# A decoder block on one core: a fourth step of eight by seven products in 15 wide blocks, one of the weight sums by an adding transfer, PSUM banks in pairs

## The chip, the core and the metric

The kernel runs on one core of a Trainium2 chip. The metric is the device time of one execution in microseconds, the median of several runs. All inputs and weights lie in HBM when it starts and the output is in HBM when it ends.

## The reference

One layer of a decoder on 256 positions with 2048 features, all in float32. `w_in` has 17408 columns, and the feed-forward part has 5632 hidden features.

```python
a = rmsnorm(h, norm_mix_pre)
q_a, k_a, v_a, q_r, f_r, i_r, g_r, gate_a, gate_r = split_columns(a @ w_in)
attn  = ...   # dilated window attention, three groups, mixed by their softmax denominators
r_out = ...   # gated linear recurrence, normed per head, times silu(g_r)
y = sigmoid(gate_a) * (attn @ w_attn_branch) + sigmoid(gate_r) * (r_out @ w_hgrn_branch)
h = h + rmsnorm(y @ w_mix_out, norm_mix_post)
a = rmsnorm(h, norm_ffn_pre)
gt, up = split(a @ w_ffn_gate_up)
h = h + rmsnorm((silu(gt) * up) @ w_ffn_down, norm_ffn_post)
```

## The kernel before

All products are made in float32r. To keep float32 accuracy each operand is split into a high part (ACT copies it to float32r) and a low part (VectorE subtracts the high part from the original), and a product is three matmuls: high by high, high by low, low by high. Every weight is used for one pass over the 256 positions, so it has to be loaded (SP), split (ACT and VectorE) and multiplied (PE) once, and the program is one long list of such steps, `seq`. Three raw buffers (`N_RAW`) and three buffers of high parts (`N_SPLIT`) turn round; while PE works on step n, `ahead(n)` emits the split of step n + 2 (`AHEAD`) and then the load that reuses the raw buffer of step n + 2, which is that of step n + 5.

The columns that need no rotation are handled in wide blocks (`Wide`, made by `add_seven`): eight of `w_in` (two column groups of 512 each: the gates, the values, the recurrence's input), two of `w_mix_out`, ten of `w_ffn_gate_up` (512 gate columns with their 512 up columns) and two of `w_ffn_down`. A wide block has two sides of 128 positions and two groups of 512 columns, so four outputs, called (0,0), (0,1), (1,0) and (1,1) by side and group. One step of a block takes 256 rows of the weights, loaded by two transfers of 512 KB, one for each group. It is a product of two matrices of two by two parts. A step by eight makes the eight products of parts, 24 matmuls of 512 columns. A step by seven makes it in the way of Strassen and Winograd with seven products, 21 matmuls: three go straight into an output, four go into shared sums called p1, p5, p6 and p7, which have banks of their own. It needs four sums of the activations (`pair_sums`, made once for each pair of rows, `x7` and `h7`) and four of the weights (made at every such step on VectorE, `sum`), and both the sums and three of the weights' parts have to be split. When the last step by seven of a block is done, `gather` combines the four shared sums into four tiles `e`; when the block is done, the evacuation adds the outputs to them (lines 674, 1106, 1327 and 1374), applies the activation, and stores the result to HBM (`kept`, from the queue of POOL) or turns it (`turn_act`, eight transposes on PE).

The list `EIGHT` gives the order of a block's eight steps as pairs of row index and kind (1 is by seven): three are by seven in each of the 18 blocks of `w_in` and gate_up, and the last step is by eight. Outputs and shared sums take four banks each; the next block swaps the two groups of banks (`flip`). PE, ACT, VectorE and POOL run their instructions in the order in which the program emits them.

Of the kernel before, what the change touches and what calls it, by code (L numbers as in the profile page):

```python
# [19 lines left out]
P = 128  # L20
# [19 lines left out]
DOWN = [[(m, m in by7) for m in range(KF // 2)] for by7 in (range(4, 20, 3), range(3, 19, 3))]  # L40

N_RAW, N_SPLIT, AHEAD, WARM, BRIDGE, LATER = 3, 3, 2, 8, 6, 16
# [21 lines left out]
class Wide:  # L64
# [7 lines left out]
    def __init__(self, w, cols, order, xs, seven, evac, prep=None, pre=None, post=None, turn=None):  # L72
        self.w, self.cols, self.order, self.xs, self.seven = w, cols, order, xs, seven
        self.evac, self.prep, self.pre, self.post, self.turn = evac, prep, pre, post, turn
        self.last7 = max((i for i, (m, s) in enumerate(order) if s), default=None)
        self.steps = len(order)
        self.bank, self.open, self.rest, self.flip, self.at = {}, set(), None, False, {}


class Step:  # L80
# [5 lines left out]
    def __init__(self, block, i, unit, half):  # L86
        self.block, self.i, self.unit, self.half = block, i, unit, half
        self.raw = self.parts = None
        self.home = None
# [4 lines left out]
def tile_hybrid_block(ctx: ExitStack, tc: tile.TileContext, t, out):  # L94
# [7 lines left out]
    accp = ctx.enter_context(tc.tile_pool(name="accp", bufs=4, space=PSUM))  # L102
    auxp = ctx.enter_context(tc.tile_pool(name="auxp", bufs=4, space=PSUM))
# [14 lines left out]

    def aux():
        return auxp.tile([P, 512], F32, tag="aux", name=nm("aux"))  # L120

    def acc_bank():
        return accp.tile([P, 512], F32, tag="acc", name=nm("acc"))
# [4 lines left out]
    def eslot(s="e"):  # L128
        return p3(s, F32, 512, 6, "e")
# [91 lines left out]
    def add_seven(*args, flip, **kw):  # L221
        b = Wide(*args, **kw)
        b.flip = flip
# [23 lines left out]
    def load(u, half):  # L247
# [9 lines left out]
        if type(b) is Wide:  # L257
            m = b.order[i][0]
            for g, col in enumerate(b.cols):
# [4 lines left out]
                )  # L264
            return
# [18 lines left out]
    def sumslot(dtype=F32R):  # L284
        return p3("sum", dtype, 2048, 1)
# [4 lines left out]
    def split(st, only=None):  # L290
        if type(st.block) is Wide:
            split_wide(st)
# [35 lines left out]
    def split_wide(st):  # L328
# [6 lines left out]
        if not by7:  # L335
            nc.scalar.activation(hi, raw, AF.Copy)  # L336
            next(prep, None)
            nc.vector.tensor_sub(lo, raw, hi.bitcast(F32))  # L338
            st.parts = hi, lo
            return  # L340
        s, d = sumslot(F32), raw[:, 512:]
        nc.vector.tensor_sub(  # L342
            s[:, :1024].rearrange("p (a c) -> p a c", a=2),
            raw[:, 512:1536].rearrange("p (a c) -> p a c", a=2),
            raw[:, None, :512].to_broadcast([P, 2, 512]),
        )
        nc.scalar.activation(hi[:, :1024], s[:, :1024], AF.Copy)  # L347
        nc.vector.tensor_add(s[:, 1024:1536], raw[:, 512:1024], s[:, 512:1024])
        nc.vector.tensor_sub(s[:, 1536:], raw[:, 1536:], s[:, 1024:1536])  # L349
        nc.scalar.activation(hi[:, 1024:], s[:, 1024:], AF.Copy)  # L350
        next(prep, None)
        dhi, dlo = (p3(x, F32R, 1536, 1) for x in ("dh", "dl"))
        nc.scalar.activation(dhi, d, AF.Copy)  # L353
        for x in (slice(0, 2048),) if b.prep else (slice(0, 1024), slice(1024, 2048)):
            nc.vector.tensor_sub(lo[:, x], s[:, x], hi[:, x].bitcast(F32))  # L355
        next(prep, None)
        nc.vector.tensor_sub(dlo, d, dhi.bitcast(F32))  # L357
        st.parts = hi, lo, dhi, dlo

    def multiply_wide(st, sides=(0, 1), groups=(0, 1)):  # L360
# [3 lines left out]
        def bank(key):  # L364

            if key not in b.bank:
                b.bank[key] = aux() if b.flip == (type(key) is not tuple) else acc_bank()
            return b.bank[key]

        def prod(key, x, w, j, last=False):  # L370
            ps = bank(key)
# [16 lines left out]
        t, d, sums = w[:2], w[2:], b.seven(m)  # L388
        last = i == b.last7
        prod((0, 1), act_of(0, 1), d, 2)  # L390
        prod((0, 0), sums(3), d, 0)
        prod("p1", act_of(0, 0), d, 1, last)
        prod("p6", sums(1), t, 2, last)
        prod("p5", sums(0), t, 1, last)
        prod("p7", sums(2), t, 0, last)
        prod((1, 1), act_of(1, 1), t, 3)

    def gather(b):

        e = {k: p3("e", F32, 512, 6) for k in ((0, 1), (1, 1), (0, 0), (1, 0))}  # L400
        x = b.bank
        nc.scalar.activation(e[0, 1], x["p1"], AF.Copy)
        nc.vector.tensor_add(e[1, 1], x["p6"], e[0, 1])
        nc.vector.tensor_add(e[0, 0], x["p5"], e[1, 1])
        nc.vector.tensor_add(e[1, 0], x["p7"], e[0, 0])
        nc.vector.tensor_add(e[1, 1], x["p7"], e[1, 1])
        b.rest = e

    def seven_sums(f, dst):

        s = ptile("s").rearrange("p (n t) -> p n t", n=4)
        a11, a12, a21, a22 = f[:, 0, :P], f[:, 1, :P], f[:, 0, P:], f[:, 1, P:]
        for o, x, c, y in ((0, a21, -1.0, a22), (1, s[:, 0, :], -1.0, a11)):
            nc.vector.scalar_tensor_tensor(
                out=s[:, o, :], in0=x, scalar=c, in1=y, op0=OP.mult, op1=OP.subtract
            )
        nc.vector.tensor_sub(s[:, 2, :], a11, a21)
        nc.vector.tensor_sub(s[:, 3, :], a12, s[:, 1, :])
# [142 lines left out]
    def flush(q):  # L561
        while q:
# [107 lines left out]
    def evac_kept(key, fn):  # L670
        def go(b):
            dst, at = keep(key, 1024), [(0, 0), (0, 1), (1, 0), (1, 1)]
            for k in at:
                nc.vector.tensor_add(b.rest[k], b.bank[k], b.rest[k])
            for s, g in at:
                e = b.rest[s, g]
# [940 lines left out]
```

## Time and profile before

| what | value |
|---|---|
| median of 3 runs | 1701.86 us (1701.73 to 1702.48) |
| span of the profiled execution, first to last instruction | 1699.6 us |
| PE busy | 1689.1 us (99%) |
| DVE busy | 1423.5 us (84%) |
| ACT busy | 908.5 us (53%) |
| POOL busy | 40.5 us (2%) |
| mean granted clock of TensorE | 0.998 |
| DMA | 344.77 MB, 203 GB/s on average |

The time of a run holds a little more than the span of a profile, which counts from the first to the last instruction; the profiled execution has no time of its own beside its span. The profile names engines PE (matmuls), PEld (weight loads of PE), DVE (VectorE), ACT (ScalarE), POOL (GpSimd) and SP (whose queue issues the loads). A group is a line of the program with the tile written and the tiles read. All matmuls have one line, that of the helper `mm`.

### The profile page before, as it was taken

The numbers are of one execution on the slowest core, as the hardware profiler recorded it, in microseconds if no ns is written. First come the engines' busy times: TensorE is split into PE (matmuls) and PEld (weight loads), VectorE is DVE, ScalarE is ACT, GpSimd is POOL, SyncE is SP. The second block draws the span as 40 slices with busy tenths as digits, with TensorE's granted clock in tenths as the row PEclk, the third lists the DMA queues.
The fourth block names the chain that finished last, engine by engine and source line by source line (L and its number), as shares of the span: only waits on it lengthen the run. The fifth ranks groups of instructions, "written<-read, shape, count | busy, mean of one in ns | idle before, by whom it ended". The sixth has DMA issues, their size and how long they took to land.

```text
span 1699.6 us, 21507 instructions
## 1 busy us (share of the span) xinstructions
PE 1689.1 (99%) x8265; PEld 1420.0 (84%) x8265; DVE 1423.5 (84%) x1604; ACT 908.5 (53%) x1023; POOL 40.5 (2%) x72
## 2 busy tenths in 40 slices
PE   9999999999999999999999999999999999999997
PEld 7888888888888888888888888888888888888886
DVE  6998888886887987776668889888888888898988
ACT  6655555554535434544445575555555555565663
POOL 0000000001000000000000000000000000000000
PEclk9999999999999999999999999999999999999999
DMA  8666666667546555565457646555555555656653
GB/s 288 220 231 232 232 232 233 228 229 258 180 149 196 188 174 175 173 216 168 154 179 249 237 147 223 198 198 198 198 198 198 198 198 198 221 195 212 200 198 114
DMA packets 206614, 344.77 MB, mean 203 GB/s; under 512 B 10960, under 2 KB 77568, under 8 KB 206512
## 3 DMA queue, kind: packets, MB, share of 16 engines
q1 hardware_dynamic: 198208, 317.89, 55.7%
q0 software_dynamic: 5680, 19.60, 3.3%
q10 hardware_dynamic: 2624, 5.92, 1.0%
q8 instruction: 64, 1.05, 0.2%
q14 instruction: 38, 0.31, 0.1%
HBM read 331.83 MB, written 11.53 MB: 202 GB/s over the span
## 4 chain that ended last, share of the span: by engine, by line
PE 98%; DVE 1%; ACT 0%; issue 0%; DVEq 0%; ACTq 0%
PE acc L135 61%; PE aux L135 35%; PE aux L833 0%; PE aux L501 0%; PE acc L1295 0%; DVE fz L1422 0%; PE aux L1295 0%; PE aux L489 0%; ACT junk L1378 0%; DVE e L1374 0%; DVE w L302 0%; DVE wl L338 0%; PE aux L1033 0%; PE acc L1158 0%; DVE g L758 0%
## 5 line engine op out<-in xcount | busy, mean ns | idle before, releaser
L338 DVE TENSOR_TENSOR wl<-raw,w 128x2048 fp32r<-128x2048 f32 x134 | 306.8, 2289 | 92.3 <-ACT w L336 90.9
L135 PE MATMUL acc<-xT,w 128*128 128x256 f32 (+1 forms) x2048 | 369.8, 339 | 0.0
L135 PEld LDWEIGHTS acc<-xT,w 128*128 128x128 f32 x2048 | 312.0, 188 | 43.8
L302 DVE TENSOR_TENSOR w<-raw,w 128x1024 fp32r<-128x1024 f32 (+1 forms) x191 | 232.5, 1218 | 136.0 <-ACT w L301 135.1
L336 ACT ACTIVATE w<-raw 128x2048 fp32r<-128x2048 f32 x134 | 256.1, 1911 | 149.3 <-PE aux L135 62.6
L301 ACT ACTIVATE w<-raw 128x1024 fp32r<-128x1024 f32 (+1 forms) x191 | 200.9, 1053 | 230.2 <-PE acc L135 187.8
L135 PE MATMUL acc<-w,hT 128*128 128x512 f32 x598 | 175.5, 390 | 0.0
L347 ACT ACTIVATE w<-sum 128x1024 fp32r<-128x1024 f32 x70 | 74.4, 1063 | 186.5 <-DVE sum L342 186.5
L355 DVE TENSOR_TENSOR wl<-sum,w 128x1024 fp32r<-128x1024 f32 (+1 forms) x128 | 168.8, 1321 | 0.0
L135 PE MATMUL acc<-w,xT 128*128 128x512 f32 x536 | 155.1, 392 | 0.0
L135 PE MATMUL aux<-w,hT 128*128 128x512 f32 x430 | 135.7, 389 | 0.0
L135 PEld LDWEIGHTS acc<-w,hT 128*128 128x128 f32 x598 | 111.7, 188 | 23.2 <-DVE w L302 0.2
L357 DVE TENSOR_TENSOR dl<-raw,dh 128x1536 fp32r<-128x1536 f32 x70 | 123.0, 1758 | 8.8 <-ACT dh L353 7.2
L135 PEld LDWEIGHTS acc<-w,xT 128*128 128x128 f32 x536 | 99.9, 188 | 20.9 <-DVE w L302 0.3
L135 PE MATMUL aux<-w,xT 128*128 128x512 f32 x344 | 108.5, 389 | 0.0
L353 ACT ACTIVATE dh<-raw 128x1536 fp32r<-128x1536 f32 x70 | 103.1, 1473 | 0.0
L135 PEld LDWEIGHTS aux<-w,hT 128*128 128x128 f32 x430 | 80.7, 188 | 16.8
L135 PE MATMUL acc<-wl,hT 128*128 128x512 f32 x227 | 86.9, 390 | 0.0
L350 ACT ACTIVATE w<-sum 128x1024 fp32r<-128x1024 f32 x70 | 74.4, 1062 | 21.8 <-DVE sum L349 21.8
L342 DVE TENSOR_TENSOR sum<-raw 128x1024 f32<-128x1024 f32 x70 | 85.2, 1217 | 0.0
L135 PE MATMUL aux<-wl,hT 128*128 128x512 f32 x215 | 83.6, 389 | 0.0
L135 PE MATMUL aux<-w,a 128*128 128x512 f32 x268 | 83.6, 389 | 0.0
(293 smaller groups left out, 2776.8 us busy)
## 6 DMA issues: line engine op xcount, KB each, us to landing
raw<-in_w_in SPq DMA_DIRECT2D x271, 512.0 KB, 4.6
raw<-in_w_ffn_gate_up SPq DMA_DIRECT2D x176, 512.0 KB, 4.4
raw<-in_w_ffn_down SPq DMA_DIRECT2D x88, 512.0 KB, 4.8
raw<-in_w_mix_out SPq DMA_DIRECT2D x32, 512.0 KB, 5.3
kept<-e POOLq DMA_DIRECT2D x32, 256.0 KB, 4.2
raw<-in_w_hgrn_branch SPq DMA_DIRECT2D x16, 512.0 KB, 4.9
raw<-in_w_attn_branch SPq DMA_DIRECT2D x16, 512.0 KB, 4.5
v<-kept POOLq DMA_DIRECT2D x8, 512.0 KB, 5.7
```

The source lines that it names most:

```text
L135: nc.tensor.matmul(ps, lhsT, rhs, start=start, stop=stop, skip_group_check=True)
L301: nc.scalar.activation(wh[:, k], raw[:, k], AF.Copy)
L302: nc.vector.tensor_sub(wl[:, k], raw[:, k], wh[:, k].bitcast(F32))
L336: nc.scalar.activation(hi, raw, AF.Copy)
L338: nc.vector.tensor_sub(lo, raw, hi.bitcast(F32))
L342: nc.vector.tensor_sub(s[:, :1024].rearrange("p (a c) -> p a c", a=2), raw[:, 512:1536].rearrange("p (a c) -> p a c", a=2), raw[:, None, : ...
L347: nc.scalar.activation(hi[:, :1024], s[:, :1024], AF.Copy)
L350: nc.scalar.activation(hi[:, 1024:], s[:, 1024:], AF.Copy)
L353: nc.scalar.activation(dhi, d, AF.Copy)
L355: nc.vector.tensor_sub(lo[:, x], s[:, x], hi[:, x].bitcast(F32))
L357: nc.vector.tensor_sub(dlo, d, dhi.bitcast(F32))
```

## The change

Fifteen of the 18 blocks of `w_in` and gate_up get four steps by seven and four by eight in turn, and so end with a step by seven. The first and last of `w_in` and the first of gate_up keep three. Such a last step makes its shared products first and its outputs last; what is emitted at its end (gather, the end sums) stands ahead of the low part of the step after next.

The step by seven is written anew. Of the four sums of weights one is formed while loading: POOL issues a transfer that adds 256 KB of the first group's rows onto the first 512 columns of the raw buffer, after SP's load of that group has landed. VectorE forms the other three (512 columns and twice 512). The raw buffer is then split like that of a step by eight, and the three sums are split in the step after, out of single buffers `sum`, `dh` and `dl`. The transposes of a finished block stand between two products of a step by seven. Shared sums and outputs are allocated as pairs of banks, and gather, end sums, activations and copies take two banks in one instruction where they can. The steps by seven of the `w_mix_out` and `w_ffn_down` blocks take the new form too, with as many of them as before.

```diff
-X7 = H7 = (0, 1, 2)
+X7, H7 = tuple(range(4)), tuple(range(4))
-EIGHT = [(3, 0), (4, 0), (0, 1), (5, 0), (1, 1), (6, 0), (2, 1), (7, 0)]
+EARLY = [order(x) for x in ["88787878"] + ["87878787"] * 6 + ["88787878"]]
+FFN = [order(x) for x in ["88787878"] + ["87878787"] * 8 + ["87878787"]]
+PAIRS = ((0, 0), (0, 1)), ((1, 0), (1, 1)), ("p1", "p6"), ("p5", "p7")
...
+    def pair_of(n):
+        return banks(n, 2).tile([P, 2, 512], F32, tag=n, name=nm(n))
...
+    def four_e():
+        return p3("e", F32, 2048, 1).rearrange("p (n c) -> p n c", n=4)
...
     def load(u, half):
...
             for g, col in enumerate(b.cols):
...
+                if g == 0 and by7:
+                    rows = b.w[(2 * m + 1) * P : (2 * m + 2) * P, col : col + 512]
+                    nc.gpsimd.dma_start(raw[:, :512], rows, accum_op=OP.add)
...
     def split_wide(st):
...
+        nc.scalar.activation(hi, raw, AF.Copy)
+        yield
         next(prep, None)
-        dhi, dlo = (p3(x, F32R, 1536, 1) for x in ("dh", "dl"))
-        nc.scalar.activation(dhi, d, AF.Copy)
-        for x in (slice(0, 2048),) if b.prep else (slice(0, 1024), slice(1024, 2048)):
-            nc.vector.tensor_sub(lo[:, x], s[:, x], hi[:, x].bitcast(F32))
+        if by7:
+            w = raw.rearrange("p (n c) -> p n c", n=4)
+            flat = p3("sum", F32, 1536, 1)
+            d = flat.rearrange("p (n c) -> p n c", n=3)
+            nc.vector.tensor_sub(d[:, 0], w[:, 0], w[:, 2])
+            nc.vector.tensor_sub(
+                d[:, 1:], w[:, 1:4:2], d[:, 0:1].to_broadcast([P, 2, 512])
+            )
+            st.rest = split_sums(st, flat, prep)
+        yield
+        nc.vector.tensor_sub(lo, raw, hi.bitcast(F32))
+
+    def split_sums(st, flat, prep):
+        hi, lo = (p3(x, F32R, 1536, 1) for x in ("dh", "dl"))
+        nc.scalar.activation(hi, flat, AF.Copy)
+        yield
         next(prep, None)
-        nc.vector.tensor_sub(dlo, d, dhi.bitcast(F32))
-        st.parts = hi, lo, dhi, dlo
+        nc.vector.tensor_sub(lo, flat, hi.bitcast(F32))
+        st.parts += hi, lo
...
     def multiply_wide(st, sides=(0, 1), groups=(0, 1)):
...
-        prod((0, 1), act_of(0, 1), d, 2)
-        prod((0, 0), sums(3), d, 0)
-        prod("p1", act_of(0, 0), d, 1, last)
-        prod("p6", sums(1), t, 2, last)
-        prod("p5", sums(0), t, 1, last)
-        prod("p7", sums(2), t, 0, last)
-        prod((1, 1), act_of(1, 1), t, 3)
+        outs = (
+            lambda: prod((0, 1), act_of(0, 1), w, 3, st.last),
+            lambda: prod((0, 0), sums(3), w, 1, st.last),
+            lambda: prod((1, 1), act_of(1, 1), d, 2, st.last),
+        )
+        turn, at = None, (0, 0, 4)
+        if st.last:
+            at = 4, 4, 4
+        elif st.between:
+            turn, at = st.between(), (0, 0, 2)
+        shared = (
+            ("p1", act_of(0, 0), w, 2), ("p6", sums(2), d, 0),
+            ("p5", sums(1), d, 1), ("p7", sums(0), w, 0),
+        )
...
     def gather(b):
+        e, x = four_e(), b.bank
+        nc.scalar.activation(e[:, 1], x["p1"], AF.Copy)
+        nc.vector.tensor_add(e[:, 3], x["p6"], e[:, 1])
+        nc.vector.tensor_add(e[:, 0], x["p5"], e[:, 3])
+        nc.vector.tensor_sub(
+            e[:, 2:], e[:, 0:4:3], x["p7"][:, None, :].to_broadcast([P, 2, 512])
+        )
...
     def evac_ffn(b):
...
+        nc.vector.tensor_mul(e[:, 1:4:2], e[:, 1:4:2], e[:, 0:4:2])
...
         if n >= 2:
...
+            late = type(b) is Wide and i == b.last7 == b.steps - 1
+            if not late:
+                rest()
...
         if st.last:
             evacs.append(b.evac(b))
             advance(evacs)
+            if late:
+                rest()
```

In `ahead` the emission for step n is now: the high part of the sums of step n + 1, the high part of step n + 2, at a block's first step two parts of the evacuation before, the low part of the sums of n + 1, the weight sums of n + 2, its low part and the load (`rest`).

The first place is VectorE's queue where one gate_up block before follows another. In the names `raw` holds loaded weights, `w` their high and `wl` their low part, `e` the tiles of the block that ends, `aux` and `acc` the banks:

```order
L403 TENSOR_TENSOR e_8811<-acc_8667,e_8810 128x512
L404 TENSOR_TENSOR e_8812<-acc_8671,e_8811 128x512
L405 TENSOR_TENSOR e_8813<-acc_8675,e_8812 128x512
L406 TENSOR_TENSOR e_8811<-acc_8675,e_8811 128x512
L338 TENSOR_TENSOR wl_8820<-raw_8727,w_8819 128x2048
L1327 TENSOR_TENSOR e_8812<-aux_8568,e_8812 128x512
L1327 TENSOR_TENSOR e_8810<-aux_8575,e_8810 128x512
L1327 TENSOR_TENSOR e_8813<-aux_8582,e_8813 128x512
L1327 TENSOR_TENSOR e_8811<-aux_8589,e_8811 128x512
L342 TENSOR_TENSOR sum_8858<-raw_8755 128x1024
```

There a low part stands between gather and end sums, and the block's last step and the next one's first are by eight. The same place of the changed kernel, where `dl` is the low part of the three sums:

```order
L375 TENSOR_TENSOR sum_9283<-raw_9185 128x512
L376 TENSOR_TENSOR sum_9283<-raw_9185,sum_9283 128x1024
L452 TENSOR_TENSOR e_9307<-acc_9084,e_9307 128x512
L453 TENSOR_TENSOR e_9307<-acc_9103,e_9307 128x512
L454 TENSOR_TENSOR e_9307<-e_9307,acc_9103 128x1024
L463 TENSOR_TENSOR e_9307<-aux_9040,e_9307 128x1024
L463 TENSOR_TENSOR e_9307<-aux_9053,e_9307 128x1024
L381 TENSOR_TENSOR wl_9281<-raw_9185,w_9280 128x2048
L1391 TENSOR_TENSOR e_9307<-e_9307 128x2x512
L389 TENSOR_TENSOR dl_9319<-sum_9283,dh_9318 128x1536
L381 TENSOR_TENSOR wl_9322<-raw_9220,w_9321 128x2048
```

The low part of the step after next (`wl_9281`, from `raw_9185`, the next block's second step) has moved behind gather and both end sums, and the weight sums of the same step stand ahead of them.

The second place is PE at the end of such a block, from its last shared product (p7, bank `aux_8810`) to the first product of the next block:

```order
L164 MATMUL aux_8810<-w_8920,so_8427 128x512
L164 MATMUL aux_8810<-wl_8921,so_8427 128x512
L164 MATMUL aux_8810<-w_8920,so_8427 128x512
L164 MATMUL acc_8747<-w_8920,hT_7888 128x512
L164 MATMUL acc_8747<-wl_8921,hT_7888 128x512
L164 MATMUL acc_8747<-w_8920,hT_7888 128x512
L164 MATMUL acc_8747<-w_8920,so_8427 128x512
L164 MATMUL acc_8747<-wl_8921,so_8427 128x512
L164 MATMUL acc_8747<-w_8920,so_8427 128x512
L164 MATMUL acc_8760<-dh_8951,hT_7888 128x512
L164 MATMUL acc_8760<-dl_8952,hT_7888 128x512
L164 MATMUL acc_8760<-dh_8951,hT_7888 128x512
```

Three outputs of three matmuls each now stand between the last shared product and the next block, which writes its outputs to the banks of the shared sums.

More of the change, by code (lines that the diff above doesn't have):

```diff
@@ L362, in multiply_wide, with prod @@
         m, by7 = b.order[i]
-        def bank(key):
+        def prod(key, x, w, j, last=False):
             if key not in b.bank:
[L367 to L371, printed above, removed]
+                side = "aux" if b.flip == (type(key) is not tuple) else "acc"
+                if b.whole:
+                    keys = next(k for k in PAIRS if key in k)
+                    pair = b.bank[keys] = pair_of(side)
+                    b.bank.update((k, pair[:, n, :]) for n, k in enumerate(keys))
+                else:
+                    b.bank[key] = bank_of(side)
+            ps = b.bank[key]
             wh, wl = (v[:, j * 512 : (j + 1) * 512] for v in w)
@@ new lines, in multiply_wide @@
+        turn, at = None, (0, 0, 4)
[7 more added lines that the diff above has]
+        )
+        for n in range(5):
+            for out, k in zip(outs, at):
+                if k == n:
+                    out()
+            if n < 4:
+                prod(*shared[n], last)
+            if n == 0 and turn:
+                turn()
@@ L561, in flush @@
     def flush(q):
+        q = deque(q) if type(q) is list else q
         while q:
@@ L1289, in turn_act, with turn_into @@
         act_t.append(dst)
+        side = "aux" if b.flip else "acc"
+        pair = pair_of(side) if b.whole else [bank_of(side) for _ in range(2)]
+        return lambda: turn_into(dst, pair, u, b.whole)
+    def turn_into(dst, pair, u, whole):
         for i in range(2):
-            ps = aux() if b.flip else acc_bank()
+            ps = pair[:, i, :] if whole else pair[i]
             for kk in range(2):
@@ L1390, in evac_down @@
         parts = [(j, i) for i in range(2) for j in range(2)]
-        for j, i in parts:
-            down_sum(j, i, b)
+        add_up(b)
         yield
@@ L1529, in tile_hybrid_block @@
         if type(b) is Wide:
+            if i == b.turn and b.order[i][1]:
+                st.between = lambda: turn_act(turns.popleft(), b) if turns else None
             multiply_wide(st)
@@ L1537, in tile_hybrid_block @@
         if n < 2:
-            ahead(n)
+            ahead(n)()
         advance(evacs)
```

204 lines of the change are left out of this document (107 added, 97 removed).

## The prediction

> **What bounds the kernel now.** I read the page first, then the list of waits, the chain in order of time, and the stages of the wide blocks.
>
> ```profile
> span 1699.6 us, 21507 instructions
> PE 1689.1 (99%) x8265; PEld 1420.0 (84%) x8265; DVE 1423.5 (84%) x1604; ACT 908.5 (53%) x1023; POOL 40.5 (2%) x72
> PE 98%; DVE 1%; ACT 0%; issue 0%; DVEq 0%; ACTq 0%
> ```
>
> TensorE is busy 99% of the span and is 98% of the chain that ended last. The timed runs have a median of 1701.86, so 2.3 us lie around this span; I work on the span and add them back. The waits of PE alone are two:
>
> ```profile
> PE aux L135 <- DVE warm L159: 1.2, 1, 1.2
> PE aux L135 <- DVE wl L338: 0.6, 1, 0.6
> ```
>
> So nothing else holds it, and what a stage costs is its count of matmuls times their pace. The chain gives the pace (start, length, engine, count), first for a w_in block, then for a gate_up block:
>
> ```profile
> 97.94 12.24 PE acc L135 x54
> 139.42 12.24 PE aux L135 x54
> ...
> 1416.41 10.88 PE acc L135 x48
> 1427.29 0.87 PE aux L1295 x8
> 1458.78 21.76 PE aux L135 x96
> ```
>
> 12.24 / 54 is 0.2267 us for a matmul of 512 columns. A block before has 5 steps of 24 and 3 of 21, 183 in all: 41.48 us, exactly the distance from 97.94 to 139.42. A gate_up block adds the 8 transposes (0.87): 42.36, against 42.37 from 1416.41 to 1458.78. The blocks run without a gap. VectorE is next:
>
> ```profile
> 181.00:222.00 41.00, 41.00 (x183) 33.94 (x182) 35.77 (x32) 22.55 (x19) 2.17 (x4) 1.00 0.67 231
> 1160.00:1201.00 41.00, 41.00 (x187) 34.03 (x186) 36.10 (x33) 22.96 (x19) 0.00 (x0) 1.00 0.56 191
> ```
>
> The columns are span, PE, PEld, DVE, ACT and POOL busy, clock, DMA share, GB/s. VectorE works 36 of 41 us there, which leaves some 5 us a block; ACT is half idle and the clock is full.
>
> **What the change takes from PE.** In 15 of the 18 wide blocks a fourth step goes by seven products. That is 15 x 3 = 45 matmuls fewer; the instruction order has 45 fewer of 512 columns and all else on PE in the same number. 45 x 0.2267 = **10.2 us off**. A w_in block becomes 40.81 us and a gate_up block 41.68.
>
> **What it does to VectorE.** The rows:
>
> ```profile
> L338 DVE TENSOR_TENSOR wl<-raw,w 128x2048 fp32r<-128x2048 f32 x134 | 306.8, 2289 | 92.3 <-ACT w L336 90.9
> L357 DVE TENSOR_TENSOR dl<-raw,dh 128x1536 fp32r<-128x1536 f32 x70 | 123.0, 1758 | 8.8 <-ACT dh L353 7.2
> 1208.55 2.43 DVE L355 TENSOR_TENSOR wl<-sum,w 128x1024 fp32r<-128x1024 f32 x2
> L342 DVE TENSOR_TENSOR sum<-raw 128x1024 f32<-128x1024 f32 x70 | 85.2, 1217 | 0.0
> L348 DVE TENSOR_TENSOR sum<-raw,sum 128x512 f32<-128x512 f32 x70 | 48.4, 692 | 2.4
> L1327 DVE TENSOR_TENSOR e<-aux,e 128x512 f32<-128x512 f32 x20 | 12.4, 682 | 0.0
> L1333 DVE SCALAR_TENSOR_TENSOR e<-e,r2c,e 128x512 f32<-128x512 f32 x20 | 14.1, 746 | 0.0
> ```
>
> A seven step had sums of 1217 + 692 + 692 ns, a low part of 2 x 1.22 and one of 1.76, 6.8 us; one addition now goes to the DMA and it has 692 + 1217 + 2289 + 1758 ns = 5.96. A block before costs 5 x 2.29 + 3 x 6.8 = 31.9, after 4 x 2.29 + 4 x 5.96 = 33.0; gather and end sums shrink from eight 512-wide operations (5.5) to two of 512 and three of 1024 (5.0). So VectorE gets about 0.6 us more in a block that is 0.7 shorter, some 4 us remain free, and on average it does not become the bound. What decides is the order at the seam between two blocks.
>
> **The seam.** Thirteen blocks that end with a seven step are followed by a block whose second step is one too. Put t = 0 where PE starts the last step (L) of a gate_up block; PE's next steps S0 to S6 then start at 4.76, 10.20, 15.83, 21.27, 26.03, 31.47 and 36.23, the next L at 41.67. More rows, of ACT and of VectorE in order of time:
>
> ```profile
> L336 ACT ACTIVATE w<-raw 128x2048 fp32r<-128x2048 f32 x134 | 256.1, 1911 | 149.3 <-PE aux L135 62.6 <-PE acc L135 61.3 <-issue 25.3
> L353 ACT ACTIVATE dh<-raw 128x1536 fp32r<-128x1536 f32 x70 | 103.1, 1473 | 0.0
> L402 ACT ACTIVATE e<-aux 128x512 f32<-128x512 f32 x11 | 6.6, 599 | 1.7 <-PE aux L135 0.9
> 1199.37 0.69 DVE L404 TENSOR_TENSOR e<-aux,e 128x512 f32<-128x512 f32 x1
> 1200.17 0.69 DVE L405 TENSOR_TENSOR e<-aux,e 128x512 f32<-128x512 f32 x1
> 1211.14 1.76 DVE L357 TENSOR_TENSOR dl<-raw,dh 128x1536 fp32r<-128x1536 f32 x1 [0.15 <-ACT dh L353]
> ```
>
> ACT splits S1's weights when S6 has left their slot, 0.1 to 2.0, and copies p1 until 2.6. On VectorE the two weight sums of S1 hide under that. Its gather starts at 2.65; dependent operations start 0.8 apart, so 3.45, 4.25, and the 1024-wide one ends at 5.5. Two end sums of 1.22: 7.95. S1's low part, now queued behind all of these: 10.25. PE wants it for its second matmul of S1, at 10.43. Then the product of gate and up (bounded by twice 0.746; I take 1.22): 11.5, and the low part of the sums: 13.25, wanted after nine matmuls, the transposes and one more, at 13.34. Nothing has more than 0.2 us to spare and a hand-over costs up to 0.15 (the last row). I take a stall of 0.15 at each seam: 13 x 0.15 = **2.0 us on**; in the 5 of w_in, with neither product nor transposes, it is the first of these two limits alone.
>
> What is hidden has this cover: PE's S0 needs the first pair of banks at 4.76 (its gather step is over at 3.45) and the second at 7.5 (free at 5.5). Where a block with pairs is followed by one with single banks, all four must be free at S0: 5.5 against 4.76, **0.7 us on**, once; the other changes of pool stand behind steps that are long over (bounds 0 and 0.7 each). SP's load of S4 waits behind the delayed low part, until 10.25, and the load of S5 stands behind it; both land before their use. On POOL the stores of kept, which wait for ACT's end activations, stand ahead of the adding transfer of S5, whose load is not out yet. The other edits (scale of the up half dropped, table load moved, fewer and wider evictions) touch engines with slack: 0.
>
> **The adding transfer** is not in the trace. The nearest rows: a load pair of SP, then 256 KB stores and 512 KB loads from POOL's queue, each with its landing time:
>
> ```profile
> L261 SPq DMA_DIRECT2D raw<-in_w_ffn_gate_up x2: 367/419/471, 1170.6 to 1171.0; - x2
> DMA to landing us min/median/max: 3.6/4.0/4.5
> ...
> L678 POOL DMA_DIRECT2D kept<-e x32: 540/540/552, 98.7 to 390.2; - x32
> DMA to landing us min/median/max: 2.8/4.2/5.9
> ...
> L668 POOL DMA_DIRECT2D v<-kept x8: 704/716/731, 393.5 to 659.4; - x8
> DMA to landing us min/median/max: 4.1/6.0/9.2
> ```
>
> It is 256 KB on POOL's queue, so its bounds are 2.8 and 9.2 us and I take 4.2, the median of its own size and queue. Call it a. It starts when the first load of the pair has landed (3.6). The Trainium skill, "DMA: Bandwidth & Descriptors", Anatomy of one DMA, puts such a transfer at 2.0 us plus bytes over 436 GB/s, which makes an estimate of 2.6 us for this one; the row of stores does not agree, and by either the sum is the same.
>
> When must it be there? S5's slot is freed by S2's low part (after 13.25, so 15.55). Load and a: 19.2 + a. Then S5's high part 1.91, low part 2.29, the low part of its sums 1.76, S6's low part 2.29: 27.45 + a, or 31.6 where that is later: PE releases the one buffer of sums at 26.03, and 1.47 + 1.76 + 2.29 stand behind it. That frees the slot of the next S1, whose load and a end at 31.15 + 2a. ACT wants it at 41.8. So a costs nothing up to 5.3, and 2 us at each seam for every us beyond. In w_in, without product and transposes, the limit comes out at 5.5. At 4.2 there is 1.1 us of room, so **0**.
>
> Sum: 1699.6 - 10.2 + 2.0 + 0.7 = 1692.1, and with the 2.3 us around it **1694.4 us**.
>
> **Rivals.** A measurement of this kernel can tell 0.2%, 3.4 us, from no change.
>
> Slower: *the adding transfer lands late*. It reads 256 KB from memory and another 256 KB from its destination, so it may behave like the 512 KB loads of the third row, a = 6.0, their median. Then the 8 seams of gate_up stall 2 x 0.7 = 1.4 us each and the 5 of w_in 2 x 0.5 = 1.0: 16.2 us, which swallow the small stalls: 1699.6 - 10.2 + 0.7 + 16.2 + 2.3 = 1708.6. It loses from a = 5.75 on, where 13 seams give back the 9.5 us that are left. For it: half of those loads took over 6.0, and S5's transfer runs beside the load of S6. Against it: half of the stores of its size landed within 4.2 and the worst in 5.9, and only 256 KB come from HBM. The Trainium skill, "Collectives: The Full Stack", The bandwidth ceiling, says of the adding step of a collective that it runs at half the rate of a copy, because it reads two sources; that is this rival, and no run here shows it yet. Chance 0.18.
>
> No change: *VectorE's operations over two banks are slow*. No row has one. If a 1024-wide one costs two of 512 (1.38 for 1.22), the four of the seam add 0.64 us, and the stall is 0.15 + 0.64 less 0.15 of room, 0.64 each: 8.3 us instead of 2.0, 1700.7. Against it: 512 from a bank takes 682, from SBUF 692. Chance 0.10.
>
> Full gain: no seam stalls, 1699.6 - 10.2 + 2.3 = 1691.7 or slightly less. Chance 0.08. The forecast, 1692 to 1698, has 0.64.
>
> **Numbers.** Faster is the forecast and the full gain, 0.72; the same 0.10; slower 0.18. The range goes from 1690, a little below the full gain, to 1706, a = 5.9 by the slope above; outside lies the late transfer with little else.
>
> **What would show it.** PE with 45 matmuls fewer; blocks 40.8 and 41.7 us apart in the chain, plus 0 to 0.3; in PE's waits the low parts of S1 (L381, L389) a few times, tenths of a us each; adding transfers landing in 3 to 5 us; VectorE at about 37 us of 41. I am wrong if PE waits over 0.7 us at a seam, and by the late transfer if those waits lead through ACT or VectorE to the queue of POOL with landings near 6 us.

## The result, and the profile after

The changed kernel takes **1746.23 us** (1741.95 to 1749.39, 4 runs) against 1702.17 (1701.73 to 1702.74): a ratio of 1.0258, 95% interval [1.0246, 1.0271]. It is slower by 44 us where 1694.4 was forecast, and far outside the range. The profiled execution took 1745.72 us, its span is 1743.9.

The page of the changed kernel: the span, the engines, then the chain that ended last by engine and by line.

```profile
span 1743.9 us, 21581 instructions
PE 1695.9 (97%) x8220; PEld 1414.6 (81%) x8220; DVE 1416.8 (81%) x1443; ACT 914.8 (52%) x943; POOL 105.3 (6%) x141
PE 54%; DMA 16%; DVE 10%; issue 3%; ACT 2%; POOLq 0%; DVEq 0%; SPq 0%; ACTq 0%
```

PE has the 45 matmuls fewer (8220 for 8265), and VectorE's share fell from 84% to 81%, so it is not full. But the chain that ended last, PE for 98% of the span before, is now PE for 54% and DMA for 16%. PE's waits (total, times, longest) say where it stood still:

```profile
PE aux L164 <- DVE e L452: 15.3, 7, 3.4
PE acc L164 <- DVE e L452: 11.9, 6, 5.2
PE acc L164 <- DVE wl L381: 5.9, 7, 1.5
PE aux L164 <- DVE wl L381: 3.1, 5, 0.8
```

7 + 6 is 13, the number of seams. At each, S0's matmuls wait for the banks that the gather (L452) empties, and then some for S1's low part (L381). VectorE's and ACT's operations only pass on a delay. The chain in order of time (start, length) through one seam of gate_up shows whose it is:

```profile
1143.76 0.70 DVE e L452
...
1156.17 0.61 DVE sum L375
...
1160.84 3.27 DMA raw<-in_w_ffn_gate_up
...
1166.78 0.70 DVE sum L375
...
1173.42 1.56 DVE wl L381
1174.99 4.95 DMA raw<-in_w_ffn_gate_up
...
1180.15 0.59 issue
1180.75 5.51 DMA raw<-in_w_ffn_gate_up
...
1186.41 1.92 ACT w L368
1188.34 0.49 ACT e L451
...
1188.85 0.70 DVE e L452
```

S6's low part ends at 1174.98 and frees the raw buffer of the next block's S1. Its load takes 4.95, POOL starts the adding transfer 0.8 later, that takes 5.51, and only then can ACT make S1's high part. The copy of p1 (L451) stands behind that on ACT, and the gather behind the copy: this is why a late S1 is seen as S0 waiting for a bank. The chain cuts S5's transfer (1160.84) off after 3.27 us, where VectorE was done with other work; the transfer itself is longer. So for the first half of the loop I took the instructions one by one, by line and stretch: S5's load on SP's queue, S5's adding transfer on POOL, then, for comparison, that of L; each with its landing time.

```profile
L290 SPq DMA_DIRECT2D raw<-in_w_ffn_gate_up x1: 368/368/368, 1156.2 to 1156.2; - x1
DMA to landing us min/median/max: 3.8/3.8/3.8
...
L296 POOL DMA_DIRECT2D raw<-in_w_ffn_gate_up x1: 844/844/844, 1160.8 to 1160.8; - x1
DMA to landing us min/median/max: 5.9/5.9/5.9
...
L296 POOL DMA_DIRECT2D raw<-in_w_ffn_gate_up x1: 854/854/854, 1169.1 to 1169.1; - x1
DMA to landing us min/median/max: 4.3/4.3/4.3
```

From the slot free for S5 (1156.17) to S1's high part (1186.41) are 30.2 us. The prediction's formula has 24.0 for the same way (from 15.55 to 31.15 + 2 x 4.2). The 6.2 between them are two loads of 3.8 and 4.95 for twice 3.6 (1.6), two hand-overs from a load's landing to POOL of 0.8 each for none (1.6), and two adding transfers of 5.9 and 5.5 for twice 4.2 (3.0). The work between the two, from S5's high part to S6's low part, took 8.1 us where the prediction had 8.25.

### The profile page after: what moved, and what is told of

Read it like the earlier page. It is cut to its first block, busy times and chain, and to the rows that moved or that the text cites. A ratio compares the mean times of both kernels' runs of the same rounds, so it can differ in the third digit from the quotient of the medians.

```text
span 1743.9 us, 21581 instructions
## 1 busy us (share of the span) xinstructions
PE 1695.9 (97%) x8220; PEld 1414.6 (81%) x8220; DVE 1416.8 (81%) x1443; ACT 914.8 (52%) x943; POOL 105.3 (6%) x141
## 4 chain that ended last, share of the span: by engine, by line
PE 54%; DMA 16%; DVE 10%; issue 3%; ACT 2%; POOLq 0%; DVEq 0%; SPq 0%; ACTq 0%
PE acc L164 39%; PE aux L164 14%; DMA raw<-in_w_ffn_gate_up 12%; DVE wl L381 4%; DMA raw<-in_w_in 4%; ACT w L368 1%; DVE e L463 1%; DVE dl L389 1%; DVE e L454 1%; DVE sum L376 1%; DVE e L1391 0%; DVE e L452 0%; PE aux L889 0%; DVE e L453 0%; DVE sum L375 0%
## 5 line engine op out<-in xcount | busy, mean ns | idle before, releaser
L368 ACT ACTIVATE w<-raw 128x2048 fp32r<-128x2048 f32 x204 | 390.1, 1912 | 360.7 <-DMA raw<-in_w_ffn_gate_up 103.3
L381 DVE TENSOR_TENSOR wl<-raw,w 128x2048 fp32r<-128x2048 f32 x204 | 466.5, 2287 | 31.1 <-ACT w L368 28.1
L386 ACT ACTIVATE dh<-sum 128x1536 fp32r<-128x1536 f32 x85 | 126.5, 1488 | 92.5 <-DVE sum L376 67.3
L389 DVE TENSOR_TENSOR dl<-sum,dh 128x1536 fp32r<-128x1536 f32 x85 | 148.9, 1752 | 3.0 <-ACT dh L386 3.0
L375 DVE TENSOR_TENSOR sum<-raw 128x512 f32<-128x512 f32 x85 | 58.5, 688 | 114.1 <-issue 44.1
L164 PEld LDWEIGHTS acc<-w,hT 128*128 128x128 f32 x566 | 105.7, 188 | 28.5 <-DVE e L452 6.7
L376 DVE TENSOR_TENSOR sum<-raw,sum 128x1024 f32<-128x1024 f32 x85 | 104.1, 1225 | 2.9
L164 PEld LDWEIGHTS aux<-w,hT 128*128 128x128 f32 x414 | 79.2, 191 | 27.1 <-DVE e L452 10.4
L164 PE MATMUL acc<-w,a 128*128 128x512 f32 x280 | 88.3, 389 | 0.0
L164 PE MATMUL acc<-wl,hT 128*128 128x512 f32 x211 | 81.3, 393 | 3.6 <-DVE wl L381 3.6
L164 PEld LDWEIGHTS aux<-w,xT 128*128 128x128 f32 x332 | 63.7, 192 | 21.2 <-DVE e L452 7.8
```

The lines of the kernel that those rows point to most:

```text
L164: nc.tensor.matmul(ps, lhsT, rhs, start=start, stop=stop, skip_group_check=True)
L375: nc.vector.tensor_sub(d[:, 0], w[:, 0], w[:, 2])
L376: nc.vector.tensor_sub(d[:, 1:], w[:, 1:4:2], d[:, 0:1].to_broadcast([P, 2, 512]))
L386: nc.scalar.activation(hi, flat, AF.Copy)
L389: nc.vector.tensor_sub(lo, flat, hi.bitcast(F32))
```

## The experiments

Theory: the *latency in series*. A raw buffer's load, then the adding transfer, then the split stand one behind another, twice round the loop that comes back to the next S1, and what is over the room of that loop PE waits. Rivals: the *load* that adding packets put on the DMA engines; a *full VectorE* at the seam; and that fewer matmuls bring nothing. The kernel before ran beside each group at 1701.55 to 1702.24. A time without a range is that of a single run; four runs of the changed kernel lie within 7.4 us, five of e9 within 0.7.

**1. The adding transfer left out, and written plainly.**

```diff
-                    nc.gpsimd.dma_start(raw[:, :512], rows, accum_op=OP.add)   # e1: with nothing in its place
+                    nc.gpsimd.dma_start(raw[:, :512], rows)                    # e2
```

> The changed kernel without the adding transfer: the weight sum of the fourth part is left out (the first part goes in as loaded), everything else stands where it stood. Late transfer (load, hand-over and add in series hold the weights of the seam's step back, and through the raw buffers the seam after): the seams run almost without a gap, 1692 to 1697 us. Seam order (VectorE's and ACT's operations between two blocks, over two banks, are themselves too long): about as the changed kernel, over 1735.

> The same 256 KB by the same queue of POOL behind the same load, but written plainly over the first part instead of added to it (the weight sum is another one). Late transfer by its series alone: a step of some 4.2 to 4.7 us instead of 5.5, so half or more of the 44 us comes back, 1700 to 1722. If the adding itself is what is dear (its packets take the DMA engines 2.2 times as long for a byte as plain ones of this queue), the loads beside it get faster too and nearly all comes back, 1694 to 1705.

Measured: e1 **1691.83**, e2 **1706.82**. PE's waits in e1, all of them:

```profile
PE aux L164 <- DVE warm L188: 1.2, 1, 1.2
PE aux L164 <- DVE wl L378: 0.7, 1, 0.7
```

So the transfer is the whole loss, 54.4 us, and seam, pairs of banks and VectorE's order cost nothing. The same 256 KB in the same place without adding cost 15.0. The row of POOL's queue in e1 (packets, MB, share of 16 engines):

```profile
q0 software_dynamic: 5424, 19.60, 3.5%
```

The same row in e2, and the landing times of the 256 KB there:

```profile
q0 software_dynamic: 12224, 41.89, 7.7%
DMA to landing us min/median/max: 2.8/3.9/6.6
```

And in the changed kernel:

```profile
q0 software_dynamic: 17664, 41.89, 11.4%
DMA to landing us min/median/max: 4.0/5.0/8.3
```

With the rest of the queue (3.5% of 1690.0 us) taken off, the adding packets take 198.8 - 59.2 = 139.6 us of all 16 engines and the plain ones, for the same bytes, 131.3 - 59.2 = 72.1: 1.9 times. Each adding packet has 2 KB and takes 178 ns (median); plain packets of 2 KB on the queue of the loads (q1) take 84. The 39.4 us between the two kernels are 3.0 at each of 13 seams. From the issue of S5's load to the landing of the next S1's transfer the changed kernel takes 30.6 us in the mean of these seams, and e2 27.7, which is 2.9 less.

**2. The sum made by an engine.**

```diff
-                    nc.gpsimd.dma_start(raw[:, :512], rows, accum_op=OP.add)
+                    nc.gpsimd.tensor_add(raw[:, :512], raw[:, :512], raw[:, 512:1024])   # e3
+            nc.vector.tensor_add(raw[:, :512], raw[:, :512], raw[:, 512:1024])           # e4: two steps later
```

> The sum is made by GpSimd's own elementwise addition, 512 columns in SBUF behind the same load, instead of a transfer. Late transfer: some 1.5 us behind the load instead of over 6, 1692 to 1699. Seam order: over 1735. A third way: GpSimd and VectorE hold each other up at their reads of SBUF, then VectorE's subtractions get longer than 2.29 us and it lands between, 1700 to 1715.

> The sum is made by VectorE, one step ahead of the split (0.69 us more for each step by seven, 2.8 us a block), no transfer. Late transfer: VectorE keeps 1 to 2 us free in a block, some seams pay a few tenths more, 1693 to 1702. Seam order or VectorE as the bound: over 1735.

Measured: e3 **1694.65**, e4 **1759.28**, slower than with the transfer, which I had not expected. In e4 PE waits chiefly for ACT. Two of its waits:

```profile
PE aux L164 <- ACT act L1358: 20.4, 5, 4.2
PE acc L164 <- ACT act L1358: 16.9, 4, 4.2
```

And ACT in order of time, at one of them:

```profile
1186.47 1.91 ACT L365 ACTIVATE w<-raw 128x2048 fp32r<-128x2048 f32 x1 [7.21 <-DVE raw L1556]
1188.28 1.01 ACT L1358 ACTIVATE act<-aux 128x1024 f32<-128x1024 f32 x1
```

ACT stood 7.2 us for VectorE's sum before it could make a high part, and the eviction that PE needed (L1358, which only gate_up has) stood behind. Two later kernels asked whether that or a full VectorE was the cause, by leaving VectorE's sum to w_in and giving gate_up GpSimd's. The first, e12, made the first sum of w_in twice, by GpSimd and then by VectorE, so its output differs there and its 1715.54 us decide nothing; e14 has VectorE's alone.

```diff
+        if ... and seq[k].block.w is w_in:      # VectorE's sum
+                if g == 0 and by7 and b.w is not w_in:     # GpSimd's (e12: always true)
```

> As e4_dve_add (VectorE makes the first sum, 1759.28 us), but only in w_in's wide blocks; in gate_up and in the other stages GpSimd makes it as in e3_pool_add. Theory: in e4_dve_add the loss came from ScalarE, where the high part of the late sum stands ahead of the eviction of the turned blocks of gate_up, which w_in does not have: 1694 to 1698. Rival: VectorE is full wherever it makes the sum, 7 of the 15 blocks lose as they did: 1694.65 + 64.6 x 7 / 15 = 1725.

> As e12_dve_w_in was meant: that kernel made the first sum in w_in twice, by GpSimd and by VectorE; here VectorE alone makes it in w_in's wide blocks, GpSimd in gate_up and the other stages. Theory: the loss of e4_dve_add came from ScalarE's order in gate_up (the high part of a late sum ahead of the eviction of the turned blocks), which w_in does not have: 1694 to 1700. Rival: VectorE, with 0.7 us more in each of four steps, is full in w_in too, and the 7 blocks lose their share of e4_dve_add's 64.6 us, 1715 to 1725.

Measured: e14 **1696.66**, against 1694.5 for GpSimd in both. VectorE has room for the sum in w_in; the loss of e4 lies in gate_up. That it is ACT's order there is read from the rows above; moving the eviction ahead of the high part was not tried.

**3. The bytes without the chain.** e5 is e3 with the same adding transfers onto tiles that nobody reads.

```diff
                     nc.gpsimd.tensor_add(raw[:, :512], raw[:, :512], raw[:, 512:1024])
...
+                    to_side(rows)
...
+        nc.gpsimd.dma_start(two[0], rows, accum_op=OP.add)      # in to_side
```

> As e3_pool_add (GpSimd makes the sum of two blocks of weights, 1694.65 us), and beside it the 69 adding transfers of 256 KB of the wide blocks are still issued, behind GpSimd's addition, but onto two tiles of their own that nobody reads: the bytes are on the DMA engines, and out of the chain. Theory, the latency in series (load, then adding transfer, then high part): nobody waits for these transfers, so 1695 with at most 3 more, and PE's waits stay under 5 us in all. Rival, the load on the DMA engines (adding packets take 2.2 times the time of plain ones per byte, and the share of the DMA engines reaches 0.8 to 1.06 in the slices of a seam): the loads of weights land later by themselves, their median of 4.4 to 4.6 us goes to 5 and more, and a good part of the 52 us between 1694.65 and 1746.2 stays: 1705 or more.

Measured: **1697.45**, 3.0 above e9 below. The queue is as busy as in the changed kernel, the loads (second row, of L303) land 0.3 later than the median of 4.5 in e3, and PE does not wait for them:

```profile
q0 software_dynamic: 17664, 41.89, 11.5%
DMA to landing us min/median/max: 3.4/4.8/8.6
```

Issued there, with nobody waiting, the transfers cost 3 us of the 54; the rest is the wait in the chain.

**4. An earlier start.** e6 splits the first load of a seven step in two, so that the adding transfer starts when the first 256 KB are there.

```diff
+                    for k in range(2):
+                        nc.sync.dma_start(raw[:, k * 512 : (k + 1) * 512], src[k * P : (k + 1) * P])
...
```

> As the changed kernel, but the first load of a seven step (512 KB for two blocks of 128 rows) is two of 256 KB, so that the adding transfer, which needs only the first of them, starts as soon as that one has landed and runs beside the other and beside the second pair. Theory, the latency in series: the adding transfer starts about 0.5 to 1.0 us earlier, twice round the loop of a seam at 13 seams, so 13 to 26 us less than 1746: 1720 to 1733. Rival, the DMA engines' load: the same bytes in the same stretch, and a transfer that runs beside more loads lands as late as before, 1743 to 1749.

Measured: **1739.86**, 6.4 us below the changed kernel's median, where the theory had 13 to 26 and the rival 3 at most. It is one run, 2.1 below the fastest of the changed kernel, so the size of this gain is uncertain. The adding transfers of S5 and of the next S1 at a seam of e6, with their landing times; SP had issued the loads before them at 1148.85 and 1166.98:

```profile
L300 POOL DMA_DIRECT2D raw<-in_w_ffn_gate_up x1: 844/844/844, 1152.3 to 1152.3; - x1
DMA to landing us min/median/max: 6.4/6.4/6.4
...
L300 POOL DMA_DIRECT2D raw<-in_w_ffn_gate_up x1: 867/867/867, 1171.2 to 1171.2; - x1
DMA to landing us min/median/max: 7.0/7.0/7.0
```

They start 3.5 and 4.2 us after the load's issue, where the changed kernel has 4.6 and 5.75, so 1.1 and 1.55 earlier. But they take 6.4 and 7.0 for 5.9 and 5.5, since they now run beside the other loads of their own step. 0.6 are left of the first, and nothing of the second. Over all 13 seams the medians are 6.5 and 7.0 for 6.0 and 5.7. So latency in series and load on the engines can't be told apart here: beside more loads the same transfer takes longer, and that counts wherever it is waited for.

**5. Three of eight steps.** e7 and e8 put the 45 matmuls back, without and with the adding transfer.

```diff
-EARLY = [order(x) for x in ["88787878"] + ["87878787"] * 6 + ["88787878"]]
-FFN = [order(x) for x in ["88787878"] + ["87878787"] * 8 + ["87878787"]]
+EARLY = [order(x) for x in ["88787878"] * 8]
+FFN = [order(x) for x in ["88787878"] * 10]
```

> As e1_no_add (the adding transfer left out, so that part of the sum of the weights is missing; 1691.83 us), but all 18 wide blocks have three of eight steps by seven, as the kernel before: only the count of matmuls goes back by 45. Theory: the whole gain of e1_no_add is these 45 at 0.2267 us, so 1691.8 + 10.2 = 1702.0, within 1.5 of it, that is the time of the kernel before. Rival: a part of the gain comes from the other edits (pairs of banks, wider evictions, order of the last step), and the time stays below 1700.

> As the changed kernel with its adding transfers, but all 18 wide blocks have three of eight steps by seven and end with an eight step: the adding transfers are 70 instead of 85, and no block that ends by seven is followed by one whose second step is by seven. Theory, the loop of the raw buffers at the seam: between two seven steps lies always an eight step whose load needs no adding transfer, the loop has 5 us more room, and next to nothing is left of the loss: 1702 to 1708. Rival, each adding transfer costs its share wherever it stands (54.4 us over 85 of them is 0.64 us each): 1702 + 70 x 0.64 = 1747.

Measured: e7 **1701.40**, e8 **1704.78**. e7 is 9.6 above e1: the matmuls are nearly the whole gain, 10.2 by the prediction's pace. In e8 70 transfers cost 3.4 us, where 85 cost 54.4: a transfer does not have a price of its own. (The expectation says that an eight step lies between two seven steps; that holds in both kernels. The loop holds two transfers in both, too: at a seam of e8 the transfer of a block's last seven step, issued at 1141.26, holds back the low part that ends at 1155.75 and frees the buffer of the next block's first seven step, whose transfer goes out at 1160.10. What differs in the trace is the order behind it. That step is the block's third, its high part at 1166.37 comes after the gather at 1159.57, and no bank waits for it. No run changes this order alone.)

**6. Which transfers.** In the 15 blocks, e10 leaves the transfer to S3 and L and gives the other sums to GpSimd; e13 is its mirror, with the transfer at S1 and S5.

```diff
+                    if b.steps == 8 and b.whole and i in (3, 7):      # e13: (1, 5)
...
+                        nc.gpsimd.dma_start(raw[:, :512], rows, accum_op=OP.add)
+                    else:
+                        nc.gpsimd.tensor_add(raw[:, :512], raw[:, :512], raw[:, 512:1024])
```

> As e3_pool_add, but in the 15 blocks with four steps by seven the sums of the second of these steps (S3) and of the last (L) are made by the adding transfer again, 30 transfers; GpSimd makes those of S1 and S5 and of all other steps. Theory: only the two adding transfers in the loop round a seam (S5's, then that of the next S1) cost time, because S1's work waits for banks and end sums behind it; S3's and L's have an eight step's slack: 1694 to 1697, and half of VectorE's slowing goes, so that it may be a little below 1694.65. Rival: every adding transfer costs its share (54.4 us over 85 is 0.64 us each): 1694.65 + 30 x 0.6 = 1713.

> The mirror of e10_mixed: in the 15 blocks with four steps by seven the adding transfer makes the sums of S1 and S5 (30 transfers), GpSimd those of S3 and L and of all other steps. e10_mixed, with S3 and L by transfers, lost 15 us against e9_pool_add_timed. Theory A, the loop of the raw buffers round the seam holds the transfers of S5 and S1 and they are the slower ones in the trace of the changed kernel (5.5 to 6.4 us against 4.2 to 4.4): more is lost here than there, 25 to 45 us, 1720 to 1740. Theory B, one loop goes through all four sums of a block (slot, load, transfer, high part, low part, slot), so that what counts is the sum of the waits in a block and not their place: here as there, 1709 within 5, and the two losses are less than the 52 of all four because the first part of each is slack.

Measured: e10 **1709.49** (1707.0 to 1713.74; ratio 1.0045 [1.0032, 1.0058]), e13 **1753.61**, one run. The landing times of the adding transfers are 3.9/4.4/7.2 (least, median, most) in e10, and in e13, with its longest wait of PE:

```profile
DMA to landing us min/median/max: 4.6/6.1/9.1
PE acc L164 <- DVE e L455: 16.7, 6, 5.1
```

Place decides, not number: 30 transfers at S1 and S5 cost 59 us against e9, more than all four places together, and 30 at S3 and L 15. But S3 and L are not free, as I had said for e10. Two transfers of S3 and two of L, in turn, in the chain of e10:

```profile
1121.17 4.45 DMA raw<-in_w_ffn_gate_up
...
1144.60 6.09 DMA raw<-in_w_ffn_gate_up
...
1164.19 3.87 DMA raw<-in_w_ffn_gate_up
...
1187.59 6.17 DMA raw<-in_w_ffn_gate_up
```

Each comes every 43.0 us, where PE needs 41.68. L's is the one that is waited for: when it lands at 1150.69, ACT has stood 5.4 us and VectorE 2.7. From there VectorE works almost without a gap until S1's low part ends at 1169.23, and PE waits 0.75 for that.

Why e13 is worse than the changed kernel is in its trace. VectorE's work in the loop, from the landing of S5's transfer to the issue of the next S1's load, takes 9.2 to 9.4 us at its 13 seams, beside GpSimd's sum for L, and 8.3 in the changed kernel. The whole way from S5's load to the landing of S1's transfer is 31.3 in the mean for 30.6, some 8 us over 13 seams for the 7.4 between the two times. The expectation ended at 1740.

**7. A better version.** e9 times e3; e11 is e3 with a fourth seven step in two more blocks.

```diff
-EARLY = [order(x) for x in ["88787878"] + ["87878787"] * 6 + ["88787878"]]
-FFN = [order(x) for x in ["88787878"] + ["87878787"] * 8 + ["87878787"]]
+EARLY = [order(x) for x in ["88787878"] + ["87878787"] * 7]      # e11
+FFN = [order(x) for x in ["87878787"] * 10]
```

> The kernel of e3_pool_add again (GpSimd makes the first sum of the weights on the chip, in place of the adding transfer), timed against the kernel before. Theory: all 85 additions leave the DMA engines' chain and 45 matmuls stay out, 10.2 us less than before, of which GpSimd's slowing of VectorE takes back 2 to 3: 1694.6, ratio to before 0.9955 to 0.9960. Rival: the single time of e3_pool_add was a lucky one, and the ratio is 1.000 within 0.001.

> As e3_pool_add, but the last wide block of w_in and the first of gate_up have four steps by seven as well, 17 blocks in place of 15. Theory: 6 matmuls fewer, 6 x 0.2267 = 1.4 us, less the waits that a first seven step right at the start of gate_up may bring: 1693.3 to 1694.7. Rival: the weight sum of that first block's second step comes late, since three groups of single banks and their evictions stand before it, and the gain is lost: 1694.7 to 1698.

Measured: e9 **1694.47** (1693.99 to 1694.63), ratio 0.9956 [0.9943, 0.9968], the best version that computes everything; e11 1698.38, ratio 0.9981 [0.9972, 0.9990]: 6 matmuls fewer, and 3.9 us more than e9, so the rival's case. Its new waits, 2.6 us, stand at the first gate_up block, behind evictions and a low part of sums, and one of 1.3 at the end of w_in. The low parts, the largest group of VectorE (busy, mean ns), in e1:

```profile
L378 DVE TENSOR_TENSOR wl<-raw,w 128x2048 fp32r<-128x2048 f32 x204 | 466.4, 2286 | 35.1 <-ACT w L365 33.4
```

and in e9:

```profile
L380 DVE TENSOR_TENSOR wl<-raw,w 128x2048 fp32r<-128x2048 f32 x204 | 489.1, 2397 | 23.8 <-ACT w L367 23.3
```

GpSimd's sums lengthen these operations of VectorE by 22.7 us in all, and e9 is 2.6 us above e1.

## Why the prediction was wrong

- **The matmuls**: right. e1 is 10.0 to 10.4 us below the kernels before, e7 shows that nearly all of this is the 45 matmuls.
- **VectorE, the seam's order and the banks**: the 2.0 and 0.7 us on were not needed. e1 keeps the new order, and PE waits at no seam. The "no change" rival (two-bank operations of 1.38 us) falls with it; the rows of L454 and L463 in the changed kernel are 1.22.
- **The adding transfer**: this step failed, in the size of its terms and not in its mechanism. The forecast left a loop with 1.1 us of room per pass, or 2.25 in all, on a load of 3.6, a hand-over of nothing and a = 4.2. At the seam shown the way from S5's slot to S1's high part is 6.2 longer, 3.95 more than its room: 3.0 come from a, 1.6 from the loads, 1.6 from the hand-overs. The other half of the loop, from there to S2's low part, took 14.8 where the forecast had 15.4. So the gathers at 1143.76 and 1188.85 stand 45.1 apart, 3.4 more than the 41.7 of e1. The seams are not alike: by the same comparison each costs 2.5 to 6.6, and all 13 together 49 of the 54.4 us. The 3.6 was the minimum of a pair of loads, with a DMA share of 0.00 in the 3 us before them. The 4.2 was the median of plain stores (2.8 to 5.9). S3's and L's transfers did land in 4.0 to 4.3, but those of S5 and S1, the ones that count, run beside the two loads of the following step and took 4.2 to 8.3, median 6.0. The hand-over I left out, having priced those on VectorE.
- **The slower rival** named the cause, its path through ACT and VectorE to POOL's queue, and a landing of 6.0, the median at the seams. It came out at 1708.6 since it changed a alone and kept the load and the hand-over of the forecast. Its reason holds too: adding packets took 1.9 times as long as plain ones for the same bytes. The Trainium skill, "Collectives: The Full Stack", The bandwidth ceiling, puts an adding step at half the rate of a copy since it reads two sources, and the trace agrees. The 2.6 us by its "DMA: Bandwidth & Descriptors", Anatomy of one DMA, for 256 KB are below even the least of e2's plain transfers (2.8, median 3.9).
- **The gap seen at another place**: I had given S0's banks 1.3 us of cover (free at 3.45 against 4.76) and thought that S1's low part would be the first to be late. But S1's high part stands ahead of p1's copy on ACT, and S1's weight sums ahead of the gather on VectorE, so that a late raw buffer stops S0 as well.

## What to carry to other kernels

A transfer that is put between a load and its use can stand in the loop of the buffers more than once (here twice a block): price it with the landing times of loads that run beside others, add the hand-over to the queue that issues it, and multiply by the times it stands in the loop before comparing with the room. When an engine's operation is moved to a DMA to relieve that engine, look first for an idle engine near the data: GpSimd made the same sum in 1.3 to 3.5 us (median 1.5), and 7 of the 10 us came out. A change of order that depends on data arriving in time should be tried once with that data free, as in e1, to learn what the order itself is worth.

## What the runs showed of the hardware

A short wait can halve TensorE's clock for a while after it. PE's row after one wait at a seam of the changed kernel:

```profile
1144.51 0.73 PE L164 MATMUL aux<-w,hT 128*128 128x512 f32 x1 [1.86 <-DVE e L452]
```

and the stretches of 1 us there (span, PE, PEld, DVE, ACT and POOL busy, granted clock, DMA share, GB/s):

```profile
1143.00:1144.00 1.00, 0.00 (x0) 0.00 (x0) 0.45 (x2) 1.00 (x3) 0.00 (x0) 1.00 0.17 66
1144.00:1145.00 1.00, 0.49 (x1) 0.44 (x2) 0.90 (x2) 1.00 (x1) 0.68 (x1) 0.80 0.04 14
1145.00:1146.00 1.00, 1.00 (x4) 0.76 (x3) 0.97 (x2) 1.00 (x2) 0.18 (x1) 0.50 0.22 16
...
1148.00:1149.00 1.00, 1.00 (x6) 0.81 (x5) 1.00 (x2) 0.59 (x2) 0.00 (x0) 0.99 0.03 4
```

After 1.86 us without a matmul the clock is 0.50 until 1148.0, some 3.4 us from 1144.6 on, and matmuls start 0.43 us apart instead of 0.23. After the wait of 1.45 us at the next seam it stayed at 1.00. But the length of the wait alone does not decide. After a longer one it stayed at 1.00, too:

```profile
1415.43 0.50 PE L164 MATMUL aux<-w,hT 128*128 128x512 f32 x1 [2.80 <-DVE e L452]
1415.00:1418.00 3.00, 2.57 (x11) 2.13 (x12) 2.76 (x4) 2.84 (x2) 0.00 (x0) 1.00 0.60 87
```

The stretches of low clock in this trace begin at 188.9, 236.7, 325.4, 1144.6 and 1325.5, which are 14, 26, 240 and 53 times 3.413 us apart, and last 3.4 us (the first 6.8). Cut the span into cells of 3.413 us on this grid: before each stretch lies a cell in which PE stood still for 1.86 us or more. The wait of 2.80 falls on two cells, with 1.62 us in one, and one of 2.13 has 1.48. In e13 a wait of 3.06 us, 1.86 of it in one cell, lowered nothing, so the limit here is near that. The Trainium skill, "TensorE: Matmul & The Clock Gate", What's actually happening, has the two states and a window of 3.4 us, and the trace agrees with both; it has the low state after at least one idle window, where 1.86 us did here.

PE's busy time in the changed kernel is 16.5 us above e1's 1679.4 for the same 8220 matmuls: of the 53.9 us between the two spans 37.4 are idle time of PE and 16.5 longer matmuls. The low stretches add up to 20.5 us, and PE works in 19 of them at half its pace, so an estimate of 9.5 of the 16.5 is the clock's. In e2, where the clock stays at 1.00, PE's busy time is 5.8 above e1's as well; what that comes from stays open. Whether the slower matmuls lengthen the kernel by themselves, or lie in time that the loop needs anyway, no run tells.

GpSimd and VectorE stop each other for whole operations. In e9, GpSimd's sum and then VectorE in order of time:

```profile
1141.04 2.91 POOL L295 TENSOR_TENSOR raw<-raw 128x512 f32<-128x512 f32 x1 [7.78 <-DMA raw<-in_w_ffn_gate_up]
```

```profile
1141.05 1.75 DVE L388 TENSOR_TENSOR dl<-sum,dh 128x1536 fp32r<-128x1536 f32 x1
1142.72 3.38 DVE L380 TENSOR_TENSOR wl<-raw,w 128x2048 fp32r<-128x2048 f32 x1
1146.02 0.68 DVE L374 TENSOR_TENSOR sum<-raw 128x512 f32<-128x512 f32 x1
```

GpSimd's sum (1.3 alone) waits out L388 and lasts 2.91; then L380 waits for it and takes 3.38 in place of 2.28. The Trainium skill, "SBUF — State Buffer", Who interferes with whom, says that a VectorE operation with two inputs on chip and a GpSimd operation that reads there take a shared port one after the other; the rows agree.
